# Three gate blocks of the first half moved between the recurrent units

## The chip, the cores and the metric

The kernel runs on one core of one Trainium2 chip. The metric is the device time of one execution in microseconds, the median over several runs. Engines are named as in the profile: PE multiplies matrices (PEld is its loading of weights), DVE is the vector engine, ACT the scalar engine, POOL the general one, SP issues all DMAs of this kernel. "L142" is a line of the kernel.

## The reference

One decoder layer on 1024 tokens of width 1024, all in float32. The first sub-layer is a token mixer with two branches, merged by gates:

```python
h = rms_norm(x, norm1_gain) * (1 + scale1) + shift1          # adaLN from the vector c
proj = h @ w_in                                              # 1024 x 4608
rwkv_cols += (token_shift(rwkv_cols) - rwkv_cols) * tshift_mu
y_a = rwkv7_time_mix(rwkv_cols, ...)                         # 8 heads x 64, delta-rule state
y_b = sliding_window_sink_attention(q, k, v, ...)            # 8 query, 2 kv heads, window 128
gates = sigmoid(proj[..., g_lo:] + branch_gate_b)            # 2 x 1024 columns
merged = gate_a * (y_a @ w_branch_a) + gate_b * (y_b @ w_branch_b)
x = x + gate1 * (merged @ w_out)
x = x + gate2 * swiglu(rms_norm(x, norm2_gain) * (1 + scale2) + shift2)
```

The change concerns the `gates` of the first 512 tokens: when they are computed, not how.

## The kernel before

Every float32 product is made of three matmuls (`mm3`, L142 to L144): both factors are split into a high and a low part, and high x low, low x high and high x high are added up in PSUM. A weight block is loaded by one DMA into `wraw`, ACT makes the high part `whi` (L133), DVE the low part `wlo` (L134).

The mixer works on two halves of 512 tokens (`for h in range(NH)`). The input of a half, `hT`, is eight pairs of tiles (`hhi`, `hlo`) and stays in SBUF for the whole half; the next half's `hT` goes into the same buffers, so it waits for the last block that reads them. `proj_block(hT, j)` multiplies `hT` by 128 columns of `w_in`: 8 x 3 = 24 matmuls of 128x512, into the tile `pg`.

A half first makes blocks 12 and 13, then four **units**, p = 0 to 3, each two heads of the RWKV branch. A unit begins with three `shifted` projections (into the tile `rvk`, of which there are two), then `rwkv_unit` computes decays and keys (`sq` L522 and `ns` L524 are the norm of the keys), the matrices `asb` (L577), stores them to DRAM (`a_scr`, L583) and loads them back in another layout (`ai`, L608). With these a triangular system is solved on DVE, 31 pairs of instructions (`tmpi` L619, `rt` L623), here called solve 0 to solve 3. Its result goes through DRAM too (`t_scr` L629, `tt` L635, `tn` L638). Then comes a recurrence of eight steps in which PE and DVE take turns (`zs` L673, `vu` L683, `G` L691), at its end the product `pgt` (L737) and the store `ya_d` (L739). In the first half each unit also prepares a quarter of the second half's input (`prepare_x`: `xs` L241, `xT_d` L251), and in both halves it is followed by `ada_rest` (L875): eight steps that each load 256 KB of `ada_w` into one single buffer, scale it on ACT (`adaw` L884) and add it on POOL (L885).

After the four units the program gives the attention: its projection (`pgq`, 12 blocks of 256 columns), then four attention blocks of 128 tokens (`klo` L803, scores `sc` L827 and L829, masked scores and their maximum on DVE L831, scaling L848, the sum `ass` L764 of the query norm). Last in the half stand the 16 **gate blocks**: a `proj_block`, a Tanh on ACT into `gt` (L949) and a store `gates_d` (L951). They read `hT` alone and nothing of the units. The tile `gt` shares three buffers (`tm`) with the shifted projections and with the copies of the attention's projection.

Program order is not yet engine order. A list scheduler places the instructions of each engine; program order serves as priority, weight loads have a raised one. So attention and gates, which stand last in the program, are drawn forward into places where the units leave an engine free; each engine, and SP's queue of DMAs too, then runs its list strictly in that order.

## Time and profile before

| | |
|---|---|
| runs | 1656.13, 1649.59, 1655.84 us |
| median | 1655.84 us |
| profiled execution | 1638.24 us, its span 1636.5 us |
| busy over the span | PE 95%, PEld 73%, DVE 73%, ACT 43%, POOL 10% |
| granted clock of PE | 0.989 of full |

The numbers below are of the one profiled execution; times in it count from the start of the span. The first half with its gates lasts to about 433 us, the second to about 807 us, and the rest is output projections and FFN. Busy shares are means over stages with different limits, so the rows below are cut by stage. Matmuls are pipelined: one shows as 0.39 us although the next starts sooner, so a block's cost is read from the starts.

### The profile page before, as it was taken

The page shows a single profiled execution, that of the slowest core. Times are in us where ns is not written, and L with a number is a line of the kernel's source. Part 1 is how long each engine was busy: PE and PEld are TensorE (multiplying, and loading weights), DVE is VectorE, ACT ScalarE, POOL GpSimd, SP SyncE. Part 2 cuts the span into 40 slices and gives each one's busy share as a digit, 9 for nine tenths or more (in the row PEclk, how much of TensorE's full clock was granted, in tenths as well). Part 3 has the DMA queues.
Part 4 walks back from the last instruction along what each step waited for, and adds up shares of the span by engine and source line. Part 5 has one row for each costly group of instructions (what it writes and reads, how often), then busy time and mean ns, then how long its engine had stood idle before and what let it go on. Part 6 is the DMA issues. An engine that isn't in the chain of part 4 may idle for free.

```text
span 1636.5 us, 24815 instructions
## 1 busy us (share of the span) xinstructions
PE 1553.0 (95%) x8835; PEld 1195.9 (73%) x8835; DVE 1192.2 (73%) x2844; ACT 709.1 (43%) x1346; POOL 156.1 (10%) x220
## 2 busy tenths in 40 slices
PE   3978999999998999999999998999999999999998
PEld 2756776666665678667778886788888888888887
DVE  6689777877557868877368877976666677897465
ACT  6454343555744333446411566423333333444442
POOL 6223121212343000000000000000000000000000
PEclk9999999999999999999999999999999999999999
DMA  9345444544544323324583146253333232974441
GB/s 320 101 120 146 123 139 121 155 128 145 152 139 112 85 69 95 99 86 146 167 282 119 59 157 223 87 171 104 103 97 104 97 102 94 313 242 131 149 142 52
DMA packets 225502, 223.97 MB, mean 137 GB/s; under 512 B 38466, under 2 KB 162508, under 8 KB 225380
## 3 DMA queue, kind: packets, MB, share of 16 engines
q1 hardware_dynamic: 225380, 222.41, 44.4%
q8 instruction: 69, 1.13, 0.3%
q14 instruction: 53, 0.43, 0.1%
HBM read 171.73 MB, written 50.63 MB: 136 GB/s over the span
## 4 chain that ended last, share of the span: by engine, by line
PE 73%; DVE 11%; DMA 6%; ACT 4%; issue 2%; POOL 2%; SPq 1%; ACTq 0%; DVEq 0%; POOLq 0%
PE pgf L142 10%; PE pgf L143 10%; PE pgf L144 10%; PE pgo L144 6%; PE pgo L143 6%; PE pgo L142 6%; DMA adaw<-in_ada_w_dram 4%; PE pg L142 4%; PE pg L143 4%; PE pg L144 4%; PE pgq L142 1%; PE pgq L144 1%; PE pgq L143 1%; DVE rt L623 1%; DVE tmpi L619 1%
## 5 line engine op out<-in xcount | busy, mean ns | idle before, releaser
L142 PE MATMUL pg<-hhi,wlo 128*128 128x512 f32 x480 | 201.0, 421 | 2.0 <-DVE xwa L491 0.9
L143 PE MATMUL pg<-hlo,whi 128*128 128x512 f32 x480 | 198.8, 414 | 0.0
L144 PE MATMUL pg<-hhi,whi 128*128 128x512 f32 x480 | 198.2, 413 | 0.0
L144 PE MATMUL pgo<-wpart 128*128 128x512 f32 x420 | 163.9, 390 | 0.0
L143 PE MATMUL pgo<-wpart 128*128 128x512 f32 x420 | 163.8, 390 | 0.0
L142 PE MATMUL pgo<-wpart 128*128 128x512 f32 x420 | 163.3, 390 | 0.0
L133 ACT CAST whi<-wraw 128x1024 fp32r<-128x1024 f32 (+1 forms) x88 | 85.0, 967 | 98.2 <-PE pgf L144 45.0
L134 DVE TENSOR_TENSOR wlo<-wraw,whi 128x1024 fp32r<-128x1024 f32 (+1 forms) x88 | 100.9, 1146 | 26.0 <-ACT whi L133 18.0
L885 POOL TENSOR_TENSOR aacc<-aacc,adaw 128x512 f32<-128x512 f32 x64 | 90.6, 1416 | 257.6 <-ACT adaw L884 246.8
L142 PEld LDWEIGHTS pg<-hhi,wlo 128*128 128x128 f32 x480 | 92.5, 193 | 28.4 <-issue 6.7
L1066 DVE TENSOR_TENSOR u<-pgf,u 128x512 f32<-128x512 f32 x88 | 60.5, 689 | 68.0 <-PE pgf L144 67.1
L144 PEld LDWEIGHTS pg<-hhi,whi 128*128 128x128 f32 x480 | 92.8, 193 | 22.2 <-issue 3.3
L143 PEld LDWEIGHTS pg<-hlo,whi 128*128 128x128 f32 x480 | 92.9, 193 | 19.2 <-issue 1.3
L1061 ACT CAST wpart<-s 128x512 fp32r<-128x512 f32 x88 | 54.7, 622 | 111.0 <-PE pgf L144 99.8
L1061 ACT CAST wpart<-fo 128x512 fp32r<-128x512 f32 x77 | 48.0, 624 | 113.9 <-PE pgo L144 107.9
L1062 DVE TENSOR_TENSOR wpart<-fo,wpart 128x512 fp32r<-128x512 f32 x77 | 52.8, 687 | 52.4 <-ACT wpart L1061 52.3
L143 PEld LDWEIGHTS pgo<-wpart 128*128 128x128 f32 x420 | 78.8, 188 | 16.3 <-issue 0.2
L144 PEld LDWEIGHTS pgo<-wpart 128*128 128x128 f32 x420 | 78.9, 188 | 16.2
L142 PEld LDWEIGHTS pgo<-wpart 128*128 128x128 f32 x420 | 78.8, 188 | 16.2
L1061 ACT CAST wpart<-wraw 128x512 fp32r<-128x512 f32 x66 | 40.6, 622 | 101.3 <-PE pgf L144 98.6
L619 DVE SCALAR_TENSOR_TENSOR tmpi<-ai,inv,rt 128x60 f32<-128x60 f32 (+24 forms) x248 | 74.3, 300 | 10.6 <-DMA ai<-a_scr 6.9
L884 ACT ACTIVATE adaw<-adaw,vT 128x512 f32<-128x512 f32 x64 | 46.2, 722 | 73.2 <-DMA adaw<-in_ada_w_dram 67.7
(507 smaller groups left out, 3807.3 us busy)
## 6 DMA issues: line engine op xcount, KB each, us to landing
wraw<-in_w_in_dram SPq DMA_DIRECT2D x72, 512.0 KB
wraw<-in_ffn_w_dram SPq DMA_DIRECT2D x56, 512.0 KB
f_d<-fs SPq DMA_DIRECT2D x77, 256.0 KB
fo<-f_d SPq DMA_DIRECT2D x77, 256.0 KB
adaw<-in_ada_w_dram SPq DMA_DIRECT2D x64, 256.0 KB
w2t<-in_ffn_w_dram SPq DMA_DIRECT2D x44, 256.0 KB
adaw<-in_ada_w_dram SPq DMA_DIRECT2D x8, 1024.0 KB
gates_d<-gt SPq DMA_DIRECT2D x32, 256.0 KB
```

The source lines that it names most:

```text
L133: nc.scalar.copy(out=hi, in_=raw)
L134: nc.vector.tensor_tensor(out=lo, in0=raw, in1=hi.bitcast(F32), op=ALU.subtract)
L142: nc.tensor.matmul(ps, lhsT=ll, rhs=rh, start=first, stop=False, skip_group_check=more)
L143: nc.tensor.matmul(ps, lhsT=lh, rhs=rl, start=False, stop=False, skip_group_check=more)
L144: nc.tensor.matmul(ps, lhsT=lh, rhs=rh, start=False, stop=last, skip_group_check=more)
L619: nc.vector.scalar_tensor_tensor(out=tv, in0=ai[:, jj, j + 1:32].unsqueeze(1).broadcast_to([P, m, n]), scalar=inv2[:, j:j + 1], in1=rt[:, ...
L623: nc.vector.tensor_tensor(out=rt[:, 0:m, j + 1:32], in0=rt[:, 0:m, j + 1:32], in1=tv, op=ALU.add)
L884: nc.scalar.activation(out=wt, in_=wt, func=AF.Copy, scale=vcol("c", k))
L885: nc.gpsimd.tensor_tensor(out=acc, in0=acc, in1=wt, op=ALU.add)
L1061: nc.scalar.copy(out=hi, in_=src)
L1062: nc.vector.tensor_tensor(out=lo, in0=src, in1=hi.bitcast(F32), op=ALU.subtract)
L1066: nc.vector.tensor_tensor(out=out, in0=x, in1=y, op=op)
```

## The change

A table says how many gate blocks are given after each unit: in the first half one after unit 0 and two after unit 1, in the second none. The body of the gate loop becomes a function, and the loop at the end of the half makes the gates that have not been made, in the first half 13 instead of 16. Everything that is computed, and the number of instructions, tiles and DMAs, stays the same. Lines of the changed kernel are one higher than before up to the gate function.

```diff
@@ -26,6 +26,7 @@
 RW = 512
 NP = 4
 NPOOL = 3
+GATES_BETWEEN = ((1, 2, 0, 0), (0, 0, 0, 0))
 NC = HALF // 64
 DFF = 2816
 NJ = DFF // P
@@ -892,7 +893,16 @@
                 else:
                     attention_block(4 * h + b)
 
+        def gate(h, hT, j):
+            ps = proj_block(hT, 20 + j)
+            gt = mw.tile([P, HALF + 1], F32, tag="tm", name="gt", bufs=3)
+
+            nc.scalar.activation(out=gt[:, 0:HALF], in_=ps, func=AF.Tanh, scale=0.5,
+                                 bias=hbg[:, j:j + 1])
+            nc.sync.dma_start(out=gates_d[h, j], in_=gt[:, 0:HALF])
+
         for h in range(NH):
+            done = set()
             if h == 0:
                 hT = hT0
             else:
@@ -926,6 +936,10 @@
                     prepare_x(p)
                 ada_rest(4 * h + p)
 
+                for _ in range(GATES_BETWEEN[h][p]):
+                    gate(h, hT, len(done))
+                    done.add(len(done))
+
             if h == NH - 1:
                 wkx.close()
                 act2 = ctx.enter_context(tc.tile_pool(name="act2", bufs=NB, side="right"))
@@ -943,12 +957,8 @@
                     nc.scalar.activation(out=xT1[k], in_=xT1[k], func=AF.Identity,
                                          scale=sc1[:, k:k + 1], bias=sh1[:, k:k + 1])
             for j in range(16):
-                ps = proj_block(hT, 20 + j)
-                gt = mw.tile([P, HALF + 1], F32, tag="tm", name="gt", bufs=3)
-
-                nc.scalar.activation(out=gt[:, 0:HALF], in_=ps, func=AF.Tanh, scale=0.5,
-                                     bias=hbg[:, j:j + 1])
-                nc.sync.dma_start(out=gates_d[h, j], in_=gt[:, 0:HALF])
+                if j not in done:
+                    gate(h, hT, j)
         ysb.append(load_y(yb_d, 1, stage))
```

Because priority is program order, the scheduler also places what stands around the gates anew. On PE the first gate now stands just ahead of unit 1's three blocks, and the second and third between unit 1's and unit 2's blocks; behind the last `pgt` product of unit 3 stand four gates, before five. Where unit 2 of the second half begins, both orders have come together again and stay the same to the end. Three places of the order are used in the prediction.

SP's queue around the loads `ai` of unit 1 and the stores `t_scr` of unit 0, first before:

```order
L608 DMA ai<-a_scr 128x1x512
L241 DMA xs<-in_x_dram 128x1024
L127 DMA wraw<-in_w_in_dram 128x4x256
L608 DMA ai<-a_scr 128x1x512
L629 DMA t_scr<-rt 256x1x32 x4
L883 DMA adaw_2021<-in_ada_w_dram 128x512
```

and now:

```order
L584 DMA a_scr<-asb_1530 32x8x32 x2
L584 DMA a_scr<-asb_1531 32x8x32 x2
L128 DMA wraw<-in_w_in_dram 128x8x128
L630 DMA t_scr<-rt 256x1x32 x4
L609 DMA ai<-a_scr 128x1x512 x2
L884 DMA adaw_2051<-in_ada_w_dram 128x512
L636 DMA tt_475<-t_scr 32x8x32
L128 DMA wraw<-in_w_in_dram 128x8x128
```

Both loads `ai` of unit 1 stood ahead of the stores `t_scr` of unit 0; now they stand behind them.

SP's queue around the loads `ai` of unit 2 and the store `ya_d` of unit 0, before:

```order
L583 DMA a_scr<-asb_2197 32x8x32 x2
L883 DMA adaw_2718<-in_ada_w_dram 128x512
L583 DMA a_scr<-asb_2198 32x8x32 x2
L608 DMA ai<-a_scr 128x1x512 x2
L883 DMA adaw_2722<-in_ada_w_dram 128x512
L255 DMA xT<-xT_d 128x3x512
L739 DMA ya_d<-yt_1184 128x512
```

and now:

```order
L584 DMA a_scr<-asb_2299 32x8x32 x2
L884 DMA adaw_2824<-in_ada_w_dram 128x512
L584 DMA a_scr<-asb_2300 32x8x32 x2
L755 DMA qkv_d<-qst 128x256
L884 DMA adaw_2828<-in_ada_w_dram 128x512
L740 DMA ya_d<-yt_1184 128x512
L609 DMA ai<-a_scr 128x1x512 x2
```

The loads `ai` of unit 2, which stood right behind that unit's `a_scr` stores, now stand behind the store `ya_d` of unit 0 as well.

DVE inside solve 3 (pairs `tmpi`, `rt`; `klo`, `apr` and `amx` are attention block 0), before:

```order
L623 TENSOR_TENSOR rt<-rt,tmpi 128x29
L803 TENSOR_TENSOR klo_531<-pkT,kdup_529 64x128
L619 SCALAR_TENSOR_TENSOR tmpi<-ai,inv_2877,rt 128x28
L623 TENSOR_TENSOR rt<-rt,tmpi 128x28
L619 SCALAR_TENSOR_TENSOR tmpi<-ai,inv_2877,rt 128x54
L803 TENSOR_TENSOR klo_532<-pkT,kdup_530 64x128
L623 TENSOR_TENSOR rt<-rt,tmpi 128x2x27
L619 SCALAR_TENSOR_TENSOR tmpi<-ai,inv_2877,rt 128x52
L623 TENSOR_TENSOR rt<-rt,tmpi 128x2x26
L619 SCALAR_TENSOR_TENSOR tmpi<-ai,inv_2877,rt 128x50
L831 ISA apr,amx<-sc,band 128x128
L831 ISA amx 128x1
```

and now, from the pair with the same width:

```order
L624 TENSOR_TENSOR rt<-rt,tmpi 128x29
L620 SCALAR_TENSOR_TENSOR tmpi<-ai,inv_2979,rt 128x28
L624 TENSOR_TENSOR rt<-rt,tmpi 128x28
L620 SCALAR_TENSOR_TENSOR tmpi<-ai,inv_2979,rt 128x54
L624 TENSOR_TENSOR rt<-rt,tmpi 128x2x27
L620 SCALAR_TENSOR_TENSOR tmpi<-ai,inv_2979,rt 128x52
L624 TENSOR_TENSOR rt<-rt,tmpi 128x2x26
L135 TENSOR_TENSOR wlo<-wraw,whi 128x1024
L620 SCALAR_TENSOR_TENSOR tmpi<-ai,inv_2979,rt 128x50
L639 STREAM_TRANSPOSE tn<-tt_475 128x256
L135 TENSOR_TENSOR wlo<-wraw,whi 128x1024
L624 TENSOR_TENSOR rt<-rt,tmpi 128x2x25
```

The attention's `klo` and masked scores are gone from between the pairs. They stand behind solve 3 now; until its end only low parts of weights, steps of the recurrence of unit 2 and the norm of attention block 0 are mixed in. In solve 2 the attention's `ass` is gone in the same way, and the store `ya_d` of unit 1 on SP now stands ahead of the stores `t_scr` of unit 2 (before, between them).

## Rows read from the trace of the kernel before

**Rows 1.** Windows: length, busy us of PE, PEld, DVE, ACT, POOL; clock, DMA.

```profile
74.00:165.00 91.00, 76.46 (x371) 52.83 (x372) 79.11 (x223) 49.86 (x84) 28.88 (x46) 0.95 0.45 120
165.00:264.00 99.00, 96.87 (x958) 74.85 (x956) 78.09 (x261) 41.82 (x85) 20.08 (x22) 1.00 0.44 129
264.00:392.00 128.00, 121.71 (x942) 79.88 (x940) 94.20 (x340) 65.17 (x143) 23.96 (x21) 0.97 0.49 140
392.00:433.00 41.00, 39.09 (x180) 28.36 (x179) 24.78 (x69) 26.03 (x54) 10.48 (x10) 1.00 0.55 165
433.00:535.00 102.00, 91.40 (x447) 65.33 (x448) 67.05 (x144) 50.80 (x89) 35.66 (x45) 0.97 0.44 125
```

**Rows 2.** Waits of PE from 74 to 264 us: total, times, longest.

```profile
PE ns L524 <- ACT sq L522: 8.3, 3, 6.1
```

**Rows 3.** Timeline of ACT: start, duration, instruction, idle before and releaser.

```profile
117.61 0.72 ACT L884 ACTIVATE adaw<-adaw,vT 128x512 f32<-128x512 f32 x1 [4.17 <-DMA adaw<-in_ada_w_dram]
```

**Rows 4.** Waits of PE from 264 to 433 us.

```profile
PE sc L827 <- DVE klo L803: 4.3, 1, 4.3
```

**Rows 5.** Timeline of PE inside a gate block.

```profile
395.66 0.39 PE L142 MATMUL pg<-hhi,wlo 128*128 128x512 f32 x1
...
397.29 0.40 PE L143 MATMUL pg<-hlo,whi 128*128 128x512 f32 x1
```

**Rows 6.** Tiles `pgt` and `gt`, first half: ns (min/median/max), first, last start.

```profile
L737 PE MATMUL pgt<-sgx,gu x8: 591/592/1089, 219.6 to 391.8; 128*128 128x512 f32 x8
L949 ACT ACTIVATE gt<-pg,hbg x16: 667/687/691, 279.2 to 433.7; 128x512 f32<-128x512 f32 x16
```

**Rows 7.** Timeline of SP's issues, three stretches around the solves.

```profile
152.99 2.61 SPq L629 DMA_DIRECT2D t_scr<-rt  x4
...
215.71 1.16 SPq L608 DMA_DIRECT2D ai<-a_scr  x2
...
222.32 0.41 SPq L739 DMA_DIRECT2D ya_d<-yt  x1
...
268.25 1.27 SPq L629 DMA_DIRECT2D t_scr<-rt  x2
271.34 0.36 SPq L739 DMA_DIRECT2D ya_d<-yt  x1
...
273.08 1.13 SPq L608 DMA_DIRECT2D ai<-a_scr  x2
```

**Rows 8.** Timeline of DVE: solves 1, 2, 3 begin, last `asb`, solve 2 ends.

```profile
152.16 0.25 DVE L619 SCALAR_TENSOR_TENSOR tmpi<-ai,inv,rt 128x31 f32<-128x31 f32 x1 [0.84 <-DMA ai<-a_scr]
...
221.62 0.25 DVE L619 SCALAR_TENSOR_TENSOR tmpi<-ai,inv,rt 128x31 f32<-128x31 f32 x1 [0.16 <-DMA ai<-a_scr]
...
264.91 0.68 DVE L577 TENSOR_TENSOR asb<-pa,amask 128x512 f32<-128x512 f32 x1
...
267.80 0.42 DVE L625 TENSOR_TENSOR rt<-rt,inv 128x256 f32<-128x256 f32 x1
...
280.33 0.25 DVE L619 SCALAR_TENSOR_TENSOR tmpi<-ai,inv,rt 128x31 f32<-128x31 f32 x1 [0.48 <-DMA ai<-a_scr]
```

**Rows 9.** DVE by line, 281-320 us (solve 3): busy us, mean ns, idle before.

```profile
L134 DVE TENSOR_TENSOR wlo<-wraw,whi 128x1024 fp32r<-128x1024 f32 x3 | 3.6, 1216 | 0.0
L831 DVE CUSTOM_DVE_ANT_0 apr<-sc,band 128x128 f32<-128x128 f32 x8 | 2.3, 284 | 0.3 <-PE sc L829 0.2
L848 DVE TENSOR_SCALAR apr<-apr,aden 128x128 f32<-128x128 f32 x4 | 1.1, 276 | 0.0
L764 DVE TENSOR_REDUCE ass<-asq 128x10 f32<-128x640 f32 x1 | 0.8, 810 | 0.0
L831 DVE DVE_READ_ACCUMULATOR2_ANT amx<- 128x1 f32 x8 | 0.6, 81 | 0.0
L803 DVE TENSOR_TENSOR klo<-pkT,kdup 64x128 fp32r<-64x128 f32 x2 | 0.6, 288 | 3.7 <-ACT kdup L802 3.7
```


## The prediction

> **What bounds the kernel now.** I read the windows first, cut at the places the change touches [rows 1]. From 74 to 165 us (units 0 and 1 of the first half, up to the first recurrence) PE is busy 76.46 of 91 us: 14.5 us stand open, and DVE is the fuller engine with 79.11. From 165 to 264 PE has 96.87 of 99, 2.1 open. From 264 to 392, up to the last product of unit 3, it has 121.71 of 128, 6.3 open. From 392 to 433 come mostly gate blocks, five by the order: PE has 39.09 of 41, so this piece lasts as long as PE's work lasts. From 433 to 535, the start of the second half, 91.40 of 102, 10.6 open. Up to the product of unit 3 the open time is 14.5 + 2.1 + 6.3 = 22.9 us.
>
> Next, what ends these gaps. In the first two windows PE waits 8.3 us in three pieces for `sq`, one of them 6.1 us [rows 2]. The 6.1 us were no lack of arithmetic: ACT held a step of `ada_rest` at the head of its queue for 4.17 us until its DMA had landed, at 117.61 us; the square could only follow it [rows 3]. In the later stretch the longest wait, 4.3 us, is a score product for `klo` of the first attention block [rows 4].
>
> Last, what a gate costs. Where PE is full, its matmuls start 0.233 us apart (seven steps from 395.66 to 397.29) [rows 5]; a gate has 24, so 24 x 0.233 = 5.6 us, and three have 16.8 us. Unit 3's last product starts at 391.8 us, the last gate's Tanh at 433.7 [rows 6]; the second half can't begin before.
>
> **The change, part by part.** No matmul, weight block, Tanh or DMA is added or removed; the three gates and all that they bring (three weight loads, three `whi`, three `wlo`, three stores) are issued earlier. What the change can win is PE's open time, at most the 16.8 us of the gates.
>
> *Gate 0.* It stands in PE's order just ahead of unit 1's three blocks, where PE later has the 6.1 us wait. 5.6 us of work that waits only for weights fit under it. This is cover for moving a gate, and counts below as the reason why PE has room, not as a gain of its own.
>
> *The tail.* By the order, unit 3's last product is followed by four gates instead of five. In a stretch that is full of PE work this is one gate: **-5.6 us**. Bounds: -5.6, and 0 if unit 3's end is as much later.
>
> *Unit 3's end* is where units 2 and 3 carry the rest, so I follow their solves. (a) Solve 2 begins at 221.62 [rows 8], 5.9 us after its `ai` load was issued at 215.71 [rows 7]. In the new order that load stands behind the store `ya_d` of unit 0, which was issued at 222.32, with 0.41 us of its own. Issued at 222.7 it lands 5.9 us later: **+7.0 us**. Bounds: 0, if unit 0 finishes sooner, and 7.0. (b) Between the pairs of solve 2 the attention's `ass` (0.8 us, [rows 9]) no longer stands: **-0.8**. (c) From the end of solve 2 (267.80 + 0.42) to solve 3 were 12.1 us: `t_scr` issued at 268.25, `ai` 4.8 us later at 273.08 because a store `ya_d` (271.34) stood between, landing 7.2 us on, at 280.33 [rows 7, 8]. In the new order that store stands ahead of the solve's end; left are four `t_scr` issues and two weight loads, 4 x 0.63 + 2 x 0.4 = 3.3 us (a load taken like the store's 0.41): **-1.5** (4.8 - 3.3). (d) In solve 3 the first attention block's softmax stood between the pairs; in the new order it stands behind. What leaves: `klo` 0.6 and the wait of 3.7 ahead of it, the masked scores 2.3 + 0.3, the read of their maxima 0.6, the scaling 1.1 [rows 9]: **-8.6**. Bounds: 0, if the same place fills with other work, and -8.6. Sum for unit 3's end: +7.0 - 0.8 - 1.5 - 8.6 = **-3.9 us**. PE must do the same work up to there in 3.9 us less; 22.9 us are open, 6.1 of them in the gap that gate 0 fills.
>
> *Unit 1.* Its `ai` load now stands behind the `t_scr` stores of unit 0: solve 0's store was issued at 152.99 and takes 2.61, so the load lands at about 152.99 + 2.61 + 5.9 = 161.5, and solve 1, which began at 152.16 [rows 7, 8], is up to 9.3 us later. I count nothing: unit 1 holds unit 3 up through the `rvk` buffers, but unit 3's `asb` was done by 264.91 + 0.68 = 265.6 and its `ai` issued only at 273.08 [rows 7, 8]; these 7.5 us and the 7.0 of (a) together exceed 9.3. The cover ends if unit 2 is not late.
>
> *Attention behind the last gate.* One gate leaves the tail, and both orders meet again at unit 2 of the second half, so 5.6 us of PE work (attention blocks 2 and 3) slide behind the last gate. 10.6 us stand open there. Bounds 0 and +5.6; I take a third, **+2**, since most of it should fall into open time.
>
> *SP and `tm`.* Each early store `gates_d` waits for a Tanh at the head of SP's queue, with `a_scr` of unit 0 behind the first one. Its Tanh comes right after 24 matmuls that need nothing of the unit, so I expect it done before `a_scr`'s data: 0. If not, unit 0 starts late, which is inside the last rival's price.
>
> Sum: -3.9 - 5.6 + 2 = **-7.5 us**. The profiled execution took 1638.24 us (span 1636.5) and would take 1630.7. The runs have a median of 1655.84, 17.6 above it; I carry the difference over: **1648 us**.
>
> **The rivals.** *No change: DVE takes what PE gets.* From 74 to 165 DVE has 87% and from 264 to 392 74% (94.20 of 128), the weight loads of PE (PEld) 58% and 62% [rows 1]. If DVE sets those stretches, the gates' three `wlo` at 1.22 us each [rows 9] go into the fuller engine, +3.7; the solves give nothing back because DVE does the same work in another order, 0 in place of -3.9; the tail stays -5.6 and the attention +2. Sum +0.1: 1656. For it: DVE's share. Against it: the longest gaps of PE end with ACT, not with DVE [rows 2]. The Trainium skill, page "Perfetto Trace Analysis", section "Identifying the Most-Contended Engine", speaks for this rival: it wants TensorE judged by its weight loads and not by busy matmuls, and the fullest engine bettered first. By that rule DVE is the engine of these stretches and a shift of matmuls wins nothing there; the trace agrees as to the shares, but in the tail PEld still has 69% against DVE's 60%, so there even this rule leaves the -5.6.
>
> *The whole of it.* The three gates fill PE's gaps, units and attention are as before: -16.8, 1639. For it: 22.9 us open. Against it: `ai` of unit 2 behind `ya_d`. The same page, section "Optimization Strategy", says that kernels whose fullest engine changes over time may gain from interleaving such stretches; that is this case, and [rows 1] shows the change from DVE to PE.
>
> *Slower: SP's order holds the units.* The load `ai` of unit 2 behind `ya_d` costs its 7.0 us, solves 2 and 3 get no shorter since DVE fills up with other work, two `wlo` of gates 1 and 2 lengthen solve 0 by 2.4 us where DVE is 87% busy, the attention costs its whole 5.6 behind the last gate, and the tail gives 5.6: +9.4, 1665. It decides once solves 2 and 3 give back less than 1.1 us (9.4 - 8.3) of the 10.9 claimed above. For it: SP issues strictly in order. Against it: the softmax does leave solve 3 by the order.
>
> That the change does not do what it says is ruled out: the order has the gates where the table puts them.
>
> **How the numbers follow.** A measurement of this kernel can tell about 0.5%, 8.3 us, from no change. The forecast case has 0.54 and spreads from about -16 to 0: 0.30 beyond 8.3 us, 0.24 within. The whole gain has 0.12, all faster. No change has 0.16. Slower has 0.18, of it 0.16 beyond 8.3 us. Faster 0.30 + 0.12 = 0.42; same 0.24 + 0.16 + 0.02 = 0.42; slower 0.16. The range reaches from a little beyond the whole gain, since the start level of the runs already differs by 6.5 us (1649.59 to 1656.13), to just under the slower case: 1633 to 1664.
>
> **What would show it right or wrong.** Right: three Tanh of gates before 200 us; the 6.1 us wait for `sq` shorter or gone; solve 2 at about 228.6, solve 3 at about 285 and some 8 us shorter; unit 3's product near 388, the last gate's Tanh near 424, and the start of unit 2 in the second half 8 us earlier than before, with everything behind it shifted alike. Wrong: the Tanh at 424 but the gain gone by the second half's unit 2 (attention paid in full); solve 3 as long as before (the no-change rival); solve 1 or 2 late and PE standing before their products (the slower one); PE open less than 10 us up to unit 3's end (the whole gain). If the time differs where both orders are the same, behind unit 2 of the second half, none of these reasons holds.

## The result and the profile after

| | before | after |
|---|---|---|
| median of the first comparison (4 runs each) | 1655.25 us (1649.59 to 1656.13) | 1666.51 us (1665.80 to 1672.46) |
| profiled execution | 1638.24 us | 1672.46 us |
| span, mean granted clock of PE | 1636.5 us, 0.989 | 1670.6 us, 0.964 |

The ratio is 1.011, with an interval of 1.0072 to 1.0147: slower by 0.7 to 1.5%, where 8 us less had been forecast. These two medians alone stand at 1.007; the four runs of before were long ones, as 86 later runs of it have a median of 1646.70 us, and against those the change costs 19.8 us, 1.2%. The medians, ratios and intervals of the experiments below leave out two runs that took over 1.5% more than the fastest of their kernel, one of `ada_pool` (1703.44 us) and one of `tt_first` (1668.10 us). The spans of the two profiled executions lie 34.1 us apart, more than the medians; why is shown below.

The same cuts as in [rows 1], moved to the same events of the new trace (end of unit 3's product at 423, last gate's Tanh at 458, start of unit 2 of the second half at 568):

```profile
74.00:165.00 91.00, 76.39 (x373) 55.79 (x373) 70.77 (x203) 44.77 (x76) 23.14 (x35) 0.93 0.46 121
165.00:264.00 99.00, 97.48 (x777) 63.71 (x778) 67.89 (x215) 42.02 (x81) 20.08 (x25) 0.79 0.38 107
264.00:423.00 159.00, 149.08 (x1105) 105.05 (x1105) 108.08 (x374) 64.84 (x137) 28.20 (x26) 0.86 0.43 128
423.00:458.00 35.00, 33.79 (x154) 24.20 (x153) 21.71 (x65) 23.03 (x49) 9.93 (x7) 1.00 0.52 161
458.00:568.00 110.00, 99.06 (x484) 69.53 (x483) 79.09 (x175) 58.78 (x111) 35.26 (x49) 0.97 0.41 122
```

Up to unit 3's product PE stands open 14.6 + 1.5 + 9.9 = 26.0 us, before it was 22.9: three gates were moved forward and nothing was filled. New is the clock column: 0.79 and 0.86 where 1.00 and 0.97 stood. Only the piece from 423 to 458 is shorter than before, 35 us against 41.

The longest wait of PE from 74 to 264 us, where [rows 2] had 8.3 us for `sq` (total, times, longest):

```profile
PE pv L645 <- DVE tn L639: 5.9, 1, 5.9
```

The waits for `sq` have shrunk from 8.3 to 0.3 us, as forecast. Instead PE waits once, 5.9 us, for `tn`, the result of solve 0 on its way through DRAM. It comes at the same time as before:

```profile
152.55 0.41 DVE L625 TENSOR_TENSOR rt<-rt,inv 128x256 f32<-128x256 f32 x1
...
165.03 0.44 DVE L638 STREAM_TRANSPOSE tn<-tt 128x256 f32<-128x256 f32 x1
```

(DVE of the kernel before: end of solve 0, and `tn` of unit 0), and after the change, with the first pairs of solves 1 to 3 that answer to [rows 8]:

```profile
146.22 0.43 DVE L626 TENSOR_TENSOR rt<-rt,inv 128x256 f32<-128x256 f32 x1
...
156.19 0.25 DVE L620 SCALAR_TENSOR_TENSOR tmpi<-ai,inv,rt 128x31 f32<-128x31 f32 x1 [3.10 <-DMA ai<-a_scr]
...
162.68 0.75 DVE L492 SCALAR_TENSOR_TENSOR rvk<-pg,ommu,tm 128x512 f32<-128x512 f32 x1 [2.51 <-ACT tm L490]
...
164.88 0.44 DVE L639 STREAM_TRANSPOSE tn<-tt 128x256 f32<-128x256 f32 x1
...
240.84 0.65 DVE L620 SCALAR_TENSOR_TENSOR tmpi<-ai,inv,rt 128x31 f32<-128x31 f32 x1
...
289.12 0.43 DVE L626 TENSOR_TENSOR rt<-rt,inv 128x256 f32<-128x256 f32 x1
...
307.18 0.25 DVE L620 SCALAR_TENSOR_TENSOR tmpi<-ai,inv,rt 128x31 f32<-128x31 f32 x1 [9.53 <-DMA ai<-a_scr]
```

Solve 0 now ends 6.3 us sooner (146.22, before 152.55), but `tn` comes at 164.88 (165.03): 18.7 us behind the solve's end instead of 12.5. SP's issues show what lies between; first before, then after:

```profile
155.70 0.55 SPq L883 DMA_DIRECT2D adaw<-in_ada_w_dram  x1
...
158.16 0.39 SPq L127 DMA_DIRECT2D wraw<-in_w_in_dram  x1
158.72 1.85 SPq L635 DMA_DIRECT2D tt<-t_scr  x4
```


```profile
146.67 2.61 SPq L630 DMA_DIRECT2D t_scr<-rt  x4
149.39 1.14 SPq L609 DMA_DIRECT2D ai<-a_scr  x2
...
151.23 0.33 SPq L636 DMA_DIRECT2D tt<-t_scr  x1
153.11 0.38 SPq L128 DMA_DIRECT2D wraw<-in_w_in_dram  x1
153.53 7.17 SPq L636 DMA_DIRECT2D tt<-t_scr  x3
...
232.68 0.32 SPq L740 DMA_DIRECT2D ya_d<-yt  x1
233.17 1.16 SPq L609 DMA_DIRECT2D ai<-a_scr  x2
...
292.11 0.62 SPq L630 DMA_DIRECT2D t_scr<-rt  x1
295.13 2.92 SPq L128 DMA_DIRECT2D wraw<-in_w_in_dram  x2
298.10 1.89 SPq L630 DMA_DIRECT2D t_scr<-rt  x3
300.03 1.14 SPq L609 DMA_DIRECT2D ai<-a_scr  x2
```

Before, a step of `ada_w` (256 KB), a small store and a load of weights (512 KB) stood between the `t_scr` stores and the `tt` loads. Now the two `ai` loads of unit 1, 256 KB each, go out in between, and the three last `tt` issues take 7.17 us instead of 1.85 for four. By the semaphores that the DMAs raise in the trace, it is not the stores that were late: all four had landed by 150.6, before the first `tt` was issued. Late is what comes behind `ai`. The two `ai` loads land at 156.2 and 160.5, 6.8 and 10.5 us after their issue; `adaw`, issued behind them at 150.57, lands at 161.2, and the last `tt` at 163.5 (before, 163.0). Of the sixteen updates with which the first `tt` load reports, twelve come by 156.2 and the last four at 160.5 to 161.4, right behind the four of the second `ai` (159.7 to 160.5).

The late `adaw` holds `tn` up a second time. ACT stands at its step of `ada_rest` until 161.28, and behind that step come `tm` on ACT, then `rvk` and a `wlo` on DVE, all ahead of `tn` in their orders:

```profile
161.28 0.72 ACT L885 ACTIVATE adaw<-adaw,vT 128x512 f32<-128x512 f32 x1 [9.15 <-DMA adaw<-in_ada_w_dram]
```

That `wlo` ends at 164.77, 1.3 us behind the last landing of `tt`, and `tn` follows. Both waits stand behind the same `ai` loads; no run parts them.

SP's view shows the places of the forecast: `ya_d` of unit 0 at 232.68, `ai` of unit 2 right behind it at 233.17, and behind solve 2 two weight loads that hold SP for 2.92 us between the `t_scr` stores, with `ai` of unit 3 behind them at 300.03.

PE around its wait and behind it:

```profile
165.38 1.06 PE L645 MATMUL pv<-tn,asb 32*32 32x32 f32 x32 [5.88 <-DVE tn L639]
...
166.96 0.63 PE L145 MATMUL pg<-hhi,whi 128*128 128x512 f32 x1
...
167.81 0.63 PE L144 MATMUL pg<-hlo,whi 128*128 128x512 f32 x1
```

Behind the wait the matmuls of a block start 0.425 us apart (166.96 to 167.81, two steps) against the 0.233 of [rows 5]: PE runs at its lower level, 1.2 instead of 2.4 GHz. Two stretches show it, first before, then after:

```profile
165.00:182.00 17.00, 16.33 (x185) 12.07 (x183) 13.20 (x53) 8.16 (x18) 3.96 (x4) 0.98 0.55 157
227.00:251.00 24.00, 23.24 (x216) 17.58 (x216) 21.97 (x64) 11.35 (x23) 6.16 (x6) 1.00 0.44 129
```


```profile
160.00:165.00 5.00, 0.00 (x0) 0.00 (x0) 2.49 (x6) 3.68 (x7) 1.39 (x2) 0.70 0.27 57
165.00:182.00 17.00, 16.62 (x116) 9.55 (x116) 10.82 (x41) 7.86 (x14) 4.85 (x8) 0.50 0.40 120
227.00:251.00 24.00, 24.00 (x145) 14.96 (x145) 9.17 (x28) 9.65 (x18) 3.16 (x4) 0.50 0.36 98
```

From 165 to 182 and from 227 to 251 PE is as busy as before, at a granted clock of 0.50, and does less: 116 instructions for 185, 145 for 216. Before the clock fell PE had done nothing in the one case, no instruction from 160 to 165 us, and mostly small products in the other (`pyt`, `pk`, `zp` from 224.4 to 227). The time at half clock follows from the mean granted clock: 2 x (1 - 0.964) x 1670.6 = 120 us after, 2 x (1 - 0.989) x 1636.5 = 36 us before.

Last, unit 3's product and the gates, as in [rows 6], and what DVE waits for in solve 3:

```profile
L738 PE MATMUL pgt<-sgx,gu x8: 590/824/1061, 230.0 to 423.2; 128*128 128x512 f32 x8
L900 ACT ACTIVATE gt<-pg,hbg x16: 672/682/690, 86.0 to 458.1; 128x512 f32<-128x512 f32 x16
```


```profile
DVE zs L674 <- PE zp L671: 6.6, 6, 2.4
DVE G L692 <- PE gp L689: 6.6, 4, 2.4
DVE vu L684 <- PE up L682: 2.6, 4, 0.9
```

### The profile page after: what moved, and what is told of

Same layout as the page of the kernel before. It is cut to its first block, busy times and chain, and to the rows that moved or that the text cites. A ratio compares the mean times of both kernels' runs of the same rounds, so it can differ in the third digit from the quotient of the medians.

```text
span 1670.6 us, 24804 instructions
## 1 busy us (share of the span) xinstructions
PE 1583.7 (95%) x8835; PEld 1212.7 (73%) x8835; DVE 1198.7 (72%) x2844; ACT 709.5 (42%) x1346; POOL 154.1 (9%) x220
## 4 chain that ended last, share of the span: by engine, by line
PE 76%; DVE 9%; DMA 6%; ACT 5%; issue 3%; POOL 2%; SPq 0%; ACTq 0%; POOLq 0%; DVEq 0%
PE pgf L143 10%; PE pgf L144 10%; PE pgf L145 10%; PE pgo L144 6%; PE pgo L145 6%; PE pgo L143 6%; PE pg L145 4%; PE pg L144 4%; PE pg L143 4%; DMA adaw<-in_ada_w_dram 3%; PE pa L575 2%; PE pgq L145 1%; PE pgq L143 1%; PE yps L701 1%; PE pgq L144 1%
## 5 line engine op out<-in xcount | busy, mean ns | idle before, releaser
L145 PE MATMUL pg<-hhi,whi 128*128 128x512 f32 x480 | 203.2, 424 | 0.0
L144 PE MATMUL pg<-hlo,whi 128*128 128x512 f32 x480 | 203.0, 423 | 0.0
L135 DVE TENSOR_TENSOR wlo<-wraw,whi 128x1024 fp32r<-128x1024 f32 (+1 forms) x88 | 99.8, 1134 | 25.3 <-ACT whi L134 24.4
L144 PEld LDWEIGHTS pg<-hlo,whi 128*128 128x128 f32 x480 | 94.7, 197 | 18.7 <-DVE hlo L228 0.2
L143 PEld LDWEIGHTS pgo<-wpart 128*128 128x128 f32 x420 | 78.8, 188 | 16.2
```

The lines of the kernel that those rows point to most:

```text
L135: nc.vector.tensor_tensor(out=lo, in0=raw, in1=hi.bitcast(F32), op=ALU.subtract)
L143: nc.tensor.matmul(ps, lhsT=ll, rhs=rh, start=first, stop=False, skip_group_check=more)
L144: nc.tensor.matmul(ps, lhsT=lh, rhs=rl, start=False, stop=False, skip_group_check=more)
L145: nc.tensor.matmul(ps, lhsT=lh, rhs=rh, start=False, stop=last, skip_group_check=more)
```

## What clock and time have to do with each other

The clock also varies between runs of one and the same program. With the sixteen experiments the kernel before was run 86 times, and each run lists its time and its mean clock. The fastest took 1634.70 us with 26 us at half clock, the slowest 1658.25 us with 86 us. A straight line through the 86 points is

time = 1624.1 us + 0.393 x (time at half clock),

and the runs lie about it with a standard deviation of 1.8 us. I call it the clock line. For a variant of this kernel the half-clock time then tells what part of its loss goes with the clock, and what lies off the line. For the change the median is 92 us at half clock and 6.3 us off the line; the kernel before has 56. So of some 20 us between them, 0.393 x 36 = 14 go with the clock and 6 do not. The page "TensorE: Matmul & The Clock Gate" of the Trainium skill (section "Terms") puts the loss at the throttled time times the missing share of the clock, here 0.5; the line has 0.39, and the difference is plausible, not shown: in part of the half-clock time PE waits anyway.

The line also settles an oddity of the prediction: the profiled execution of before was 17.6 us faster than the median of the runs then known. At 36 us of half clock the line gives 1638.2. It was an execution with little half clock, and that of after one with much, so 33 of the 34 us between the profiles (0.393 x 84) go with the clock. Against the medians, 1646.70 and 1666.51, the one profile is 8.5 us short and the other 6 us long: of the 34 us some 20 are the kernel and 14 luck, and the runs decide.

## The experiments

Theories, as the expectations name them. **Q**: SP's order, `ai` of unit 2 behind `ya_d` of unit 0. **C**: the half clock of PE is what the loss consists of. **P**: unit 2's projections now stand behind unit 0's `pv`, and unit 2 is late for that. **S**: attention slides behind the last gate and is paid in the second half. **D**: unit 0's `tt` loads are late, because `ai` of unit 1 stands between them and `t_scr`; PE runs dry and the clock halves. Gates "a, b, c, d" are the numbers after units 0 to 3 of the first half.

| kernel | gates | median us (runs) | before | ratio, interval | half clock us | off the line us | solve 0's end to `tn` us |
|---|---|---|---|---|---|---|---|
| g1000 | 1, 0, 0, 0 | 1643.94 (10) | 1645.37 | 0.9983, 0.9952 to 1.0015 | 53 | -0.8 | 14.9 |
| g0200 | 0, 2, 0, 0 | 1647.20 (10) | 1645.37 | 1.0012, 0.9982 to 1.0042 | 56 | 1.3 | 13.4 |
| g0030 | 0, 0, 3, 0 | 1666.97 (4) | 1645.37 | 1.0117, 1.0068 to 1.0167 | 85 | 9.5 | 12.8 |
| ya_pool | 1, 2, 0, 0 | 1663.48 (10) | 1645.37 | 1.0110, 1.0078 to 1.0142 | 95 | 1.5 | 18.5 |
| ya_pool0 | none | 1659.92 (4) | 1644.26 | 1.0101, 1.0034 to 1.0168 | 88 | 1.8 | 12.5 |
| g2000 | 2, 0, 0, 0 | 1644.19 (10) | 1644.26 | 1.0003, 0.9975 to 1.0032 | 58 | -1.0 | 14.3 |
| g0300 | 0, 3, 0, 0 | 1665.31 (4) | 1644.26 | 1.0131, 1.0063 to 1.0199 | 78 | 11.1 | 12.9 |
| tw10 | 1, 2, 0, 0 | 1677.17 (4) | 1644.26 | 1.0186, 1.0112 to 1.0259 | 86 | 18.6 | 18.7 |
| g2100 | 2, 1, 0, 0 | 1638.97 (10) | 1644.76 | 0.9973, 0.9940 to 1.0007 | 43 | -2.3 | 12.5 |
| g0012 | 0, 0, 1, 2 | 1643.24 (10) | 1644.76 | 0.9997, 0.9969 to 1.0026 | 48 | 1.6 | 13.1 |
| attn3 | 1, 2, 0, 0 | 1662.05 (4) | 1644.76 | 1.0112, 1.0056 to 1.0169 | 83 | 5.2 | 18.9 |
| ada_pool | none | 1686.77 (3) | 1644.76 | 1.0240, 1.0173 to 1.0307 | 111 | 16.2 | 15.4 |
| tt_first | 1, 2, 0, 0 | 1652.70 (9) | 1647.18 | 1.0040, 0.9996 to 1.0084 | 63 | 2.1 | 12.5 |
| g3000 | 3, 0, 0, 0 | 1646.39 (10) | 1647.18 | 0.9995, 0.9970 to 1.0019 | 58 | -1.0 | 13.9 |
| g2100r | 2, 1, 0, 0 | 1639.92 (12) | 1647.18 | 0.9959, 0.9927 to 0.9991 | 52 | -3.2 | 12.5 |
| g2100x2 | 2, 1, 0, 0 (both halves) | 1665.90 (4) | 1647.18 | 1.0112, 1.0059 to 1.0164 | 82 | 10.7 | 12.7 |

(Medians; half clock from each run's mean clock, known to 0.001, so to about 2 us; the last column from one profile each. Those of before and of the change: 12.5 and 18.7.)

### One, two and three gates elsewhere: g1000, g0200, g0030

```diff
-GATES_BETWEEN = ((1, 2, 0, 0), (0, 0, 0, 0))
+GATES_BETWEEN = ((1, 0, 0, 0), (0, 0, 0, 0))
```

(and `(0, 2, 0, 0)`, `(0, 0, 3, 0)`.)

> Only the first gate is moved, one after unit 0; the other 15 stand at the end of the half. Here ai of unit 2 stands ahead of ya_d of unit 0 as before, but ai of unit 1 behind t_scr of unit 0. Theory Q: without ai behind ya_d the loss is gone, at most 4 us are left from unit 1 (its solve began 4.1 us later in the changed kernel), 1650 to 1659 us. Theory C: the time stands or falls with long half-clock spells of PE between 160 and 345 us; with 39 us of half clock as before it takes 1638 to 1650, with 90 us and more over 1660, whatever the SP order is.

> Only two gates are moved, both after unit 1; 14 stand at the end of the half. Here all loads ai stand as before, ahead of t_scr and of ya_d. Theory Q: no loss against the kernel before, 1640 to 1656 us, since nothing of the SP order is left. Theory C: unit 2's blocks are 11 us of PE work later and the attention's projection too, so the products behind the recurrences of units 0 and 1 still have little beside them; half-clock time over 80 us and 1660 us or more.

> Three gates as in the change, but all after unit 2; no gate between units 0, 1 and 2 by the program. Loads ai of units 1 and 2 stand as before. Theory Q: no loss, 1640 to 1657 us. Theory C: the gates stand ahead of unit 3's blocks and fill PE during the first recurrence and the wait for its tn; half-clock time at most 60 us and no loss either, 1640 to 1655. If it is as slow as the change, neither theory holds and the mere displacement of the attention is the cause.

One gate or two cost nothing: 1643.94 and 1647.20 us. Three behind unit 2 cost as much as the change, 1666.97, though its loads stand as before, which neither theory had. For Q the first two fit. For C the time goes with the half clock in all three (53, 56 and 85 us), but its forecasts of that half clock missed twice: over 80 us for g0200, at most 60 for g0030.

### The store on POOL: ya_pool, ya_pool0

```diff
-            nc.sync.dma_start(out=ya_d[h, p], in_=t1)
+            nc.gpsimd.dma_start(out=ya_d[h, p], in_=t1)
```

> The changed kernel with one edit: the store ya_d of each unit is issued by POOL instead of SP, so that the load ai of unit 2 no longer stands behind unit 0's store. Theory Q (SP's order): in the changed kernel solve 2 begins at 243.0 us, 21 us later than before, and 224.9 us is the end of unit 2's asb; freed, ai is issued at about 227 and solve 2 begins at about 234. Unit 3's end and the whole come some 9 us earlier, time about 1657 us, the half-clock time of PE (121 us in the profile of the changed kernel, 39 before) about as long as there. Theory C (clock): the time follows the half-clock time; if that stays above 80 us the kernel stays above 1660 us although solve 2 begins earlier.

> The kernel before with the store ya_d issued by POOL instead of SP, nothing else: what that edit does by itself. Every theory: within 4 us of before, as ai of unit 2 was ahead of the store already. If it is slower by 8 us or more, the run of the changed kernel with the store on POOL has hidden a gain of that size, and theory Q stands again.

The changed kernel stays slow, 1663.48 us; solve 2 begins at 238.8 instead of 240.8, not at 234. But the edit alone makes the kernel before slower by 15.7 us, which no theory had. In its profile the first half is not longer (last Tanh at 431.7, before 433.7) and the second is (to its last Tanh 385.9 us against 374.2). Why was not followed. So ya_pool can't be read as a test of Q, which by its expectation stood again, and the next pair was made.

### Gates that part Q from P: g2000, g0300

Tables `(2, 0, 0, 0)` and `(0, 3, 0, 0)`.

> Two gates, both after unit 0, 14 at the end. By the order unit 2's pz stands ahead of unit 0's pv (the product that waits for solve 0's result) as with one gate; but the load ai of unit 2 stands behind ya_d of unit 0, as in the change. Theory Q (SP's order): slower than before by 7 us or more, like the change. Theory P (unit 2's projections pushed behind unit 0's pv, and then long half-clock spells): unit 2 is not pushed, so no loss, within 5 us of before, half-clock time at most 65 us.

> Three gates, all after unit 1. By the order unit 2's pz stands behind unit 0's pv as in the change, but ai of unit 2 ahead of ya_d of unit 0 as before. Theory Q: no loss, within 5 us of before. Theory P: slower by 12 to 22 us, half-clock time 80 us or more, unit 2's last asb at about 224 us against 213 before.

Q falls on both sides: with `ai` behind `ya_d` 1644.19 us, no loss; with `ai` ahead of it 1665.31. For P the first fits, the second in time; its half clock, 78 us, lies just under the 80 forecast, and unit 2's last `asb` comes at 220.0, between the two numbers. In g0300, as in g0200, the second of unit 1's two `ai` loads stands between `t_scr` and `tt`, and `tn` is not late (12.9 and 13.4 us): one such load in between does not do what two do.

### Work for the wait: tw10

```diff
+TWICE = (10,)
...
+            if hT is hT0 and j in TWICE:
+                for k in range(KT):
+                    mm3(ps, wh[:, k, :], wl[:, k, :], hT[k][0], hT[k][1], k == 0, k == KT - 1)
             return ps
```

> The changed kernel, but the third projection block of unit 2 in the first half is multiplied twice, the second time over the first: 24 more matmuls, 5.6 us of PE work at full clock that nobody needs; ai of unit 2 is ahead of ya_d here. Theory C (the loss is half clock that follows PE's wait for tn of solve 0): part of the wait of 5.9 us is filled, the spell at 162 us shortens or goes, and the kernel takes 1655 us or less in spite of more work. Theory P without the clock (unit 2 is late, nothing else): unit 2 is later by what the block adds, so about 5 us slower than the same kernel with the store on POOL, 1668 us.

1677.17 us, and the attempt says nothing of C: the scheduler put the added pass behind `pv`. There are 328 block matmuls ahead of the first `pv` as in the change, and PE's wait is still there:

```profile
PE pv L649 <- DVE tn L643: 6.0, 1, 6.0
```

That is a finding of its own. Ahead of `pv` stand 325 block matmuls before the change and 328 after it, as if the scheduler placed there what it thinks can be done by the time `tn` comes. Here work that was given earlier did not stand there in addition, it pushed other work behind.

### Three gates that part P from S: g2100, g0012, attn3

Tables `(2, 1, 0, 0)` and `(0, 0, 1, 2)`; and in attn3 the table of the change with

```diff
-ORDER = (((), (), (), (), (-1, 0, 1, 2, 3)),
+ORDER = (((), (), (), (-1,), (0, 1, 2, 3)),
```

> Three gates, two after unit 0 and one after unit 1. By the order unit 2's pz stands behind unit 0's pv as in the change, but only 16 score products of the attention slide behind the thirtieth block (24 in the change, 10 before). Theory P (unit 2 pushed behind unit 0's pv): slow, 12 us or more over before. Theory S (the attention slides into the second half and is paid there, with the half clock that comes with it): like the two-gate kernels, within 5 us of before, and from the last gate's Tanh to unit 2 of the second half about 101 us (110 in the change).

> Three gates, one after unit 2 and two after unit 3. By the order unit 2's projections stand ahead of unit 0's pv exactly as before, but 24 score products slide as in the change. Theory P: no loss, within 5 us of before. Theory S: slow, 10 us or more over before, from the last gate's Tanh to unit 2 of the second half 109 to 113 us.

> The change itself, but the attention's projection of the first half is given ahead of unit 3 instead of behind it, so that its blocks can begin earlier: 16 score products slide instead of 24, unit 2's pz still stands behind unit 0's pv, ai of unit 2 behind ya_d of unit 0. Theory S: most of the loss goes, at most 7 us (the part that lies off the clock line) over before. Theory P: the loss stays, 12 us or more.

P's order falls by g2100: three gates, unit 2 behind `pv` as in the change, and 1638.97 us, not slower but a little faster. That a late unit 2 costs nothing is not shown by it, since unit 2 is not late there: `pv` itself comes 10 us sooner, and unit 2's last `asb` at 211.5 (before, 212.9). S falls by g0012, where as much slides (22 score products behind the last Tanh, 24 in the change), the stretch takes 108.3 us, and the kernel takes 1643.24; and by attn3, where the stretch is back to 99.8 us and the loss stays, 1662.05. What the slow attn3 has in common with the change is the column at the right of the table: 18.9 us from solve 0's end to `tn`.

### ACT's hold: ada_pool

```diff
-                nc.scalar.activation(out=wt, in_=wt, func=AF.Copy, scale=vcol("c", k))
+                nc.gpsimd.tensor_scalar(out=wt, in0=wt, scalar1=vcol("c", k), scalar2=0.0,
+                                        op0=ALU.mult, op1=ALU.add)
```

> The kernel before; the scaling step of ada_rest runs on POOL instead of ACT, so that ACT is no longer held by a load of ada_w. No gate is moved. If ACT's hold is what makes PE wait 6.1 us for sq at 119 us and 5.0 us at 510 us, both waits go, and with them the half-clock spells at 118 and 507 us (6.8 us each): the time falls by 5 to 12 us, half-clock time under 45 us. If the wait has another cause, the gaps stay and so does the time; POOL's steps then at worst hold the carries of the projections, plus 5 us or more.

1686.77 us, the worst of all, and most of the wait it was to remove is still there (PE, 74 to 264 us):

```profile
PE ns L524 <- ACT sq L522: 6.1, 3, 4.7
```

So the step of `ada_rest` on ACT explains little of the 6.1 us of [rows 2]: without it the longest wait is 4.7 us. The row showed what ACT was held by at that moment, and I took that for the cause. What else sets the wait stays open, and so does the great loss of this kernel, 16.2 us off the line.

### The loads in the other order: tt_first, g3000

```diff
             for sl in range(2):
                 ai = wk.tile([P, 16, 32], F32, tag="ai", name="ai", bufs=2)
+                if h == 0 and p == 1:
+                    nc.vector.tensor_copy(ai[:, 0, 0:1], last["tn"][:, 0, 0:1])
```

(`last["tn"]` is unit 0's `tn`; the load overwrites the copied column, so only the order changes.) g3000 is the table `(3, 0, 0, 0)`.

> The change, with one small copy on DVE from unit 0's tn into unit 1's ai tile, so that the loads ai of unit 1 come behind the tt loads of unit 0. Theory D (the tt loads are late because 256 KB loads of ai stand between them and t_scr; PE runs dry and the clock halves): tn of unit 0 comes at about 159 instead of 164.9 us, 13 us after solve 0's end; PE's wait of 5.9 us and the spell of 20.5 us at 162 go or shrink below 7 us; the time falls to 1655 us or less although solve 1 begins some 8 us later. Theory P (unit 2 behind unit 0's pv): tn comes sooner but the time stays over 1660.

> Three gates, all after unit 0; the loads ai of unit 1 stand behind the tt loads of unit 0 by themselves, unit 2's pz behind unit 0's pv, ai of unit 2 behind ya_d of unit 0. Theory D: tn of unit 0 12.5 to 15 us after solve 0's end, no half-clock spell over 10 us between 155 and 200 us, within 6 us of before or faster. Theories P and Q: slow, 10 us or more over before.

SP and DVE of tt_first, then its longest wait of PE from 74 to 264 us and three windows:

```profile
147.43 2.61 SPq L634 DMA_DIRECT2D t_scr<-rt  x4
...
151.49 0.92 SPq L640 DMA_DIRECT2D tt<-t_scr  x2
...
154.32 1.08 SPq L640 DMA_DIRECT2D tt<-t_scr  x2
...
160.14 1.21 SPq L613 DMA_DIRECT2D ai<-a_scr  x2
```


```profile
159.48 0.44 DVE L643 STREAM_TRANSPOSE tn<-tt 128x256 f32<-128x256 f32 x1
```


```profile
PE pxt L248 <- DVE xs L218: 5.4, 1, 5.4
```


```profile
160.00:165.00 5.00, 5.00 (x84) 3.28 (x83) 1.37 (x6) 2.80 (x7) 1.28 (x1) 1.00 0.51 159
165.00:182.00 17.00, 15.26 (x107) 8.87 (x107) 13.58 (x39) 7.32 (x15) 4.20 (x6) 0.90 0.53 157
236.00:282.00 46.00, 44.45 (x302) 34.62 (x303) 23.61 (x84) 12.46 (x27) 6.54 (x6) 0.52 0.35 105
```

`tn` comes at 159.48, where D had it, PE's wait for it is gone from the list, and from 160 to 165 us PE is full at full clock. (The step of `ada_w` stands ahead of `ai` here too, so both waits ahead of `tn` end sooner.) From 165 to 182 the clock is 0.90 instead of 0.50. Then from 236 to 282 it is 0.52 after all: solve 1 began at 167.0, unit 1 is late (`tn` at 238.9, in the change 215.7), and PE has its lean stretch there. In time the kernel takes 1652.70 us, below the 1655 that D had as its bound, at a ratio of 1.004 with an interval of 0.9996 to 1.0084. Against the change's 1.011 (1.0072 to 1.0147) about two thirds of the loss is gone, though the intervals still touch. Its runs spread from 1640.89 us at 39 us of half clock to 1664.93 at 100, so the second lean stretch may come in some and not in others; only one was profiled. g3000, where the loads stand behind `tt` by themselves, has no loss, 1646.39 us, though PE has a spell of 10.2 us at half clock at 166, where D allowed none over 10. That is against Q, and against P too: unit 2's projections end as late as in the change (the first `pz` behind them starts at 172.6 and 172.0).

### A version that beats both: g2100r, g2100x2

g2100r is g2100 again; g2100x2 has `(2, 1, 0, 0)` in both halves.

> The kernel with two gates after unit 0 and one after unit 1 again, more often, whether it beats the kernel before: its ratio was 0.9973 with an interval to 1.0007. If the gain is real, 3 to 7 us, the interval lies below 1; if not, the ratio comes back to within 0.002 of 1.

> The same two and one gates in both halves. If in the second half too the gates take the place of waits of PE (14.8 us idle between the last gates of the halves before), it is up to 10 us faster than with the first half alone, about 1632; if the second half's end was bound by units 2 and 3 alone, within 4 us of it; if the loads ai fall between t_scr and tt there, slower by 10 us or more.

g2100 is faster than the kernel before: in its second series, g2100r, 1639.92 against 1647.18 us, ratio 0.9959 with an interval of 0.9927 to 0.9991. The windows of g2100r from 165 us to the last Tanh, and product and gates:

```profile
165.00:264.00 99.00, 95.32 (x838) 68.17 (x837) 80.44 (x245) 46.00 (x88) 22.77 (x27) 1.00 0.46 133
264.00:399.00 135.00, 129.68 (x1035) 88.90 (x1035) 107.68 (x392) 70.92 (x159) 25.29 (x23) 1.00 0.46 136
399.00:420.00 21.00, 21.00 (x100) 14.96 (x98) 12.82 (x35) 14.11 (x29) 3.87 (x3) 1.00 0.55 171
```


```profile
L738 PE MATMUL pgt<-sgx,gu x8: 591/592/697, 216.7 to 399.1; 128*128 128x512 f32 x8
L900 ACT ACTIVATE gt<-pg,hbg x16: 668/684/696, 85.6 to 419.5; 128x512 f32<-128x512 f32 x16
```

Here the last Tanh comes earlier, as was forecast (424), but by another way: the clock is 1.00 from 165 to 420 us, and the last Tanh starts 14.2 us earlier than before (419.5, before 433.7). Unit 3's product is not earlier but 7.3 us later (399.1), and the tail behind it is 20.4 us instead of 41.9, shorter by far more than the 5.6 us of one gate. Of the 14.2 us 7.3 are left in the medians. In the second half the same table costs 26 us more than it brings (1665.90, 10.7 us off the line). It is not the delay of the first half: `tn` follows its four solves by 11.2 to 14.3 us there, before by 11.6 to 15.9. More was not taken apart.

## Why the prediction was wrong

**That 22.9 us of PE's open time could be filled** is the step that failed first. The gates did take the place of the wait for `sq`, "gate 0 fits under it" held. But the next thing PE needs is `tn` of unit 0, and it came at 164.88, no sooner than before. Open time ahead of a result that comes no sooner is not won by work moved ahead of it; it moves, and here it came together in one wait of 5.9 us. Behind that wait the clock halved for some 20 us. What the gates pushed behind it, unit 2's projections, ran there: its last `asb` came at 224.2 instead of 212.9.

**Unit 1, "I count nothing"** is the step with the cause in it. I followed the `ai` loads to solve 1 (it began 4.0 us later), found slack there, and did not ask what stands behind them in SP's queue. It was a step of `ada_w` and unit 0's `tt` loads. Solve 0 ended 6.3 us sooner and all of it was lost between its end and `tn`. tt_first shows it: `ai` put behind both, `tn` 5.4 us sooner, wait gone. Which of the two, `tt` or the held ACT, would have been enough is not shown. All four kernels in which 18 us or more lie between solve 0's end and `tn` are slow.

**(a) Solve 2 +7.0**: it was +19.2 (240.84). The forecast 7.0 for the order is in it, `ai` issued 0.5 us behind `ya_d`, but `ya_d` itself was 10.4 us late with unit 0's recurrence, whose first steps ran at half clock. By g2000 that order alone costs nothing.

**(b, c) Solve 2's length and the gap to solve 3, -0.8 and -1.5**: solve 2 takes 48.3 us instead of 46.2, and the gap is 17.6 us (289.12 + 0.43 to 307.18) instead of 12.1. I had counted the two weight loads ahead of `t_scr` at 0.4 us each; they took 2.92, and SP came to them only at 295.13: both waited for their buffer, until DVE had done the `wlo` of the block before (4.4 us in two waits of SP). Ahead of the first `t_scr` SP had stood 4.5 us at a load `xT` (L256).

**(d) Solve 3 -8.6**: +5.2 (44.0 us instead of 38.8). The softmax is gone from it, as the order says, and DVE is busy 5.4 us less. But steps of unit 2's recurrence stand there, five before and six now, and in them DVE waits 6.6 + 6.6 + 2.6 us for PE's small products, at a granted clock of 0.50 from 312 to 343; before, the same waits came to 1.3 us. The bound "0, if the same place fills with other work" was still too good.

**The tail -5.6** held: from unit 3's product to the last Tanh 34.9 us instead of 41.9, so -7.0. **The attention +2** was mis-sized: from the last Tanh to unit 2 of the second half 110.3 us instead of 101.2, so +9.1, above my bound of 5.6, which counted PE's work alone; what the rest consists of was not taken apart.

By these terms the profiles add up: unit 3's end +31.4, tail -7.0, attention +9.1, the rest of the kernel, whose order is the same, +0.6: 34.1 us. And the clock was in no term. I had seen 0.95 and 0.97 in [rows 1] and read only the busy columns; 0.393 us for each us at half clock is 14 of the 20 us between the runs and 33 of the 34 between the profiles. So these terms say where the time passed, not what cost it beside the clock.

**The rivals.** The slower one came close in time (1665) and not in its reason, SP's hold of unit 2: g2000 has that hold and no loss. The rival of no change rested on DVE as the fuller engine and on the rule of the Trainium skill, page "Perfetto Trace Analysis" (section "Identifying the Most-Contended Engine"), that busy matmuls don't measure TensorE. In the stretch from 74 to 165 DVE's share fell from 87% to 78% and `tn` came no sooner, so DVE's load did not set it. The page's warning about busy time holds here too, though its reason is that matmuls are pipelined and here it is the clock: from 227 to 251 us PE is busy 24.00 of 24 us and does two thirds of the instructions.

**What stays open.** g0030 and g0300 are slow with `tn` in time; 9.5 and 11.1 us of theirs lie off the line. Their last Tanh is not late (430.5 and 429.9, before 433.7); the loss lies behind it, first in the stretch to unit 2 of the second half (112 and 113 us, in the change 110). Why has not been tested. A late unit 2 is not parted from the late `tn` either: in all four kernels with a late `tn` unit 2's last `asb` is late too (218.6 to 224.2, before 212.9), and tt_first brings it back to 215.7 with `tn`. Against a late unit 2 alone speak g0030 and g0300, where it comes at 219.1 and 220.0 and the last Tanh is on time. That the half clock costs the time, and does not only go along with it, is argued from the matmuls' pitch and the line; no run changed the clock alone.

## What to carry to other kernels

Open time on the busiest engine can be filled only up to the next result that it must wait for: look for what sets that result before counting the open time as a gain, and follow every queue position that moves to what stands behind it, not only to its own user. Count the time at half clock (from the mean granted clock of each run) beside the busy time: here a wait of 5.9 us was followed by 20.5 us at half clock, and runs of one program can be compared by it. Where a scheduler places the work, small variants of a table differ by 1% either way: g2100 and the change differ by one gate's place and by some 25 us.

## What the runs showed of the hardware

One and the same program took 1634.70 to 1658.25 us with its mean granted clock going along, 0.39 us for each us at half clock; one profile lay 17.6 us off the median of the runs then known and 8.5 off that of 86 later ones. In two long stretches PE stayed at the lower level although it was nearly always busy (24.00 of 24 us from 227 to 251 in the change, 44.45 of 46 us from 236 to 282 in tt_first). And a load can hold up what is issued behind it: the two `ai` loads of 256 KB took 6.8 and 10.5 us to land, the `adaw` load of the same size behind them 10.6 us, where one with no `ai` ahead of it took 3.3 (tt_first, issued at 150.14), and the `tt` loads of 32 KB 5.8 to 10.2 us, before 2.9 to 3.7. How long their issue takes on SP says less: in attn3 the three last `tt` are issued in less than half the time of the change,

```profile
153.16 3.24 SPq L636 DMA_DIRECT2D tt<-t_scr  x3
```

and land at 162.8 to 163.1, with `tn` at 164.74, as late as in the change.
